# Hybrid recurrent decoder step: pairwise products alternate between two heads, two last stores on another queue, stage order changed

## The chip, the cores and the metric

One core of one Trainium2 chip runs the whole program. The metric is device microseconds of one execution. The kernel before was timed three times: 1033.18, 1036.73 and 1042.99 us, median 1036.73 us.

## The reference

One layer over a prompt of 1024 tokens and 8 single-token samples, all in float32. Each branch below has 4 heads of 64 channels, and is a causal recurrence.

```python
h = rms_norm(x, norm_g)
proj = jnp.matmul(h, w_in)            # split into the columns of four branches
o_gla  = gla_mix(q, k, v, log_a, s0)  # gated linear attention
y_s5   = s5_mix(u, ...)               # diagonal complex state space
o_gdn  = gdn_mix(q, k, v, g, beta, s0)        # gated delta net, triangular solve per 64 tokens
o_rwkv = rwkv7_mix(r, log_w, k, v, kk, a, s0) # RWKV-7
mixed = jnp.concatenate([o_gla, o_s5, o_gdn, o_rwkv]) * silu(gates)
out = rms_norm(x + mixed @ w_out, final_g)    # and the new states of every branch
```

## The kernel before, in words

The prompt is worked in two halves of 512 tokens; the second half (marked `'` in the order string) also carries the 8 sample tokens. A branch's four heads are two pairs; a pair is a *unit*, written as a generator with stages: `R` (RWKV, `rwkv_unit`), `D` (delta net, `gdn_unit`), `L` (GLA, `gla_unit`), `g` (gates), `S` (S5), `W` (weights of S5). Two heads of a pair lie on partitions 0 to 63 and 64 to 127 (`HS[0]`, `HS[1]`).

**Projections.** `stream` (L278 to L287) multiplies a 128-column weight tile with the normed tokens. Values are split in a high and a low part, so each weight block costs three matmuls of L286: `hi*hi`, `hi*lo`, `lo*hi`. In the first half a projection called before `rwkv_lora` has run is cut into two pieces of 256 columns (`X["pieces"]`, set at L129 and cleared at L418); later ones have one piece of 512. In the second half the pieces are 260 columns.

**Pairwise products.** Each of the three matrix branches builds token-by-token products per head, from 64 partitions of that head:
- RWKV, L472: for each of four blocks `b`, a PSUM tile from the pool `psb` (two tiles, tag "b"), four matmuls of one head, then a mask multiply on VectorE (L473).
- Delta net, L684: for each head a tile, eight matmuls, then a VectorE multiply (L685).
- GLA, L785 to L802: on each of six levels, for each head a tile, matmuls (L791 for the levels of 64 and 32, L794 for 16, 8, 4, 2), then ScalarE copies (L798) or VectorE predicated copies (L802).
In float32 a matmul of these is recorded as two instructions, so four matmuls of the text are x8 in the profile.

**Recurrences.** After the products a unit inverts triangular blocks (`inverse`, L296: VectorE steps L319 and L321, small DMAs, products L338, L342, L351, L356), and then steps through its chunks one after another with a 128x128 state: L515 for RWKV (eight matmuls of the program for a chunk, the state update is L531), L721 for the delta net, L851 for GLA.

**What sets the order.** `ORDER` (L33) lists stages; the loop at L1411 issues them, each under a priority offset from `PRI` (L32, by unit letter and stage number: `R1` is stage 1 of an RWKV unit, which holds L472). Within that, the tile framework orders each engine's instructions itself, by priorities and a model of when operands and buffers come free. So a few characters of the string move instructions on all engines. An engine then runs its list strictly in that order. The second half's tokens are loaded and normed by token `x'`: its transposes (L256) write into the buffers that hold the first half's tokens, so they follow the last L286 of the first half.

**The end.** `tail` (L1351) scales four row blocks of 128 tokens and one of 8, alternately on ScalarE and VectorE, and stores each (L1393) on the queue of SyncE.

Of the kernel before, what the change touches and what calls it, by code (L numbers as in the profile page):

```python
# [12 lines left out]
ALU = mybir.AluOpType  # L13
# [17 lines left out]
           rU="V", dU="V", fg="V", la="V", tlo="V", cv0="V")  # L31
PRI = {"R2": 1875, "D2": 1000, "R3": 4000, "D3": 2000, "L1": 1600, "R1": 600, "L0": 100, "L2": 600, "D0": 150, "D1": 1250}  # L32
ORDER = ("x W W t R0 m D0 W W g6 R0 W W W M D0 D1 R1 R0 R1 L0 R1 R0 L0 R1 D1 L0 g0 S g0 L1 D0 D0 g4 g6 D1 g3 g7 g2 L1 L1 D1 x' "  # L33
         "g7 g1 g5 g4 S t' R1' R1' g2 R1' m' R0' g3 M' R1' g1' g7' R0' D0' R0' D0' L1' D1' g1 g5 R0' D0' D1' g4' g6' D0' L0' L1' "
         "g2' L1' D1' g7' g0' D1' L0' g6' S' g4' L0' g5' g3' S' g5' g3' g0' g1' g2' T y T'")
GORD = ((RWKV, 0), (RWKV, 1), (GDN, 0), (GDN, 1), (GLA, 0), (GLA, 1), (S5, 0), (S5, 1))
# [27 lines left out]
def trunk(ctx: ExitStack, tc: tile.TileContext, I, O):  # L64
# [35 lines left out]
    def psb(*shape):  # L100
        return ps_b.tile(list(shape) or [128, 512], F32, tag="b", name="psb")
# [10 lines left out]
    def act(out, in_, func, scale=1.0, bias=0.0, **kw):  # L112
        A.activation(out, in_, func, bias=bias, scale=scale, **kw)  # L113
# [293 lines left out]
    def rwkv_unit(h, pair, th):  # L407
# [59 lines left out]
        Gt = [big(128, 8, 128, name="Gt") for _ in range(2)]  # L467
        for b in range(4):
            e, c0 = b % 2, 4 * (b // 2)
            pg = psb(128, 4, 128)  # L470
            for j in range(4):
                PE.matmul(pg[:, j, :], BK[HS[e], c0 + j, :], AR[HS[e], c0 + j, :], start=True, stop=True)  # L472
            gt = V.tensor_tensor(Gt[b // 2].rearrange("p (c e f) t -> p e c (f t)", f=2, e=2)[:, e], pg.rearrange("p (c f) t -> p c (f t)", f=2),  # L473
                                 maskG.rearrange("p (o t) -> p o t", o=1).to_broadcast([128, 2, 256]), ALU.mult)
        yield
# [170 lines left out]
    def gdn_unit(h, pair):  # L646
# [32 lines left out]
        act(Gt, Gt, AF.Exp)  # L679
        act(kdn, kdn, AF.Exp)  # L680
        for e in range(2):
            pg = psb(128, 4, 128)
            for c in range(8):
                PE.matmul(pg[HS[c % 2], c // 2, :], kx[HS[e], 64 * c:64 * c + 64], SK[HS[e], c, :], start=True, stop=True)  # L684
            gt = V.tensor_tensor(G4[:, e], pg, G4[:, e], ALU.mult)  # L685
        yield
# [60 lines left out]
    def gla_unit(h, pair, sm):  # L747
# [26 lines left out]
        for lv, s in enumerate((64, 32) + LEVELS[:-1]):  # L774
# [9 lines left out]
            tt("lw1", wv[:, :, 1, :], v4(qx)[:, :, 1, :], dv[:, :, 1, :])  # L784
            for e in range(2):  # L785
                pg = psb(128, 4, 64)
                for c in range(4):
                    if s >= 32:
                        for b in range(64 // s):
                            o = 128 * c + 2 * s * b  # L790
                            PE.matmul(pg[2 * s * b:2 * s * b + s, c, 0:s], W[HS[e], o:o + s], W[HS[e], o + s:o + 2 * s], start=True, stop=True)  # L791
                    else:
                        t = slice(128 * c, 128 * c + 128)
                        PE.matmul(pg[:, c, :], W[HS[e], t], W[HS[e], t].rearrange("p (b f s) -> p f b s", f=2, s=s)[:, 1], start=True, stop=True)  # L794
                if s >= 32:
# [555 lines left out]
    def tail(fgb):  # L1351
# [36 lines left out]
        for x, j, k in rows:  # L1388
            if j % 2 or j == 4:
                V.tensor_scalar(x, x, y[:k, j:j + 1], None, ALU.mult)  # L1390
            else:
                act(x, x, AF.Copy, scale=y[:k, j:j + 1])
            SP.dma_start(out=O["y"][HALF + 128 * j:HALF + 128 * j + k, :], in_=x)  # L1393

# [192 lines left out]
```

## Time and profile before

| | |
|---|---|
| median of three runs | 1036.73 us |
| profiled execution | 1045.8 us |
| its span | 1043.7 us |
| PE matmul busy | 931.7 us, 89% of the span |
| VectorE busy | 604.4 us, 58% |
| ScalarE busy | 474.7 us, 45% |
| GpSimd busy | 290.2 us, 28% |
| mean granted TensorE clock | 0.873 of 2.4 GHz |

PE is the engine that is busy nearly all the time. Its matmuls are pipelined, so its busy time counts a stretch as busy in which matmuls follow each other, whatever their rate. The profiled execution is 0.9% longer than the median, and ahead of all three timed runs.

### The profile page before, as it was taken

The numbers are of one execution on the slowest core, as the hardware profiler recorded it, in microseconds if no ns is written. First come the engines' busy times: TensorE is split into PE (matmuls) and PEld (weight loads), VectorE is DVE, ScalarE is ACT, GpSimd is POOL, SyncE is SP. The second block draws the span as 40 slices with busy tenths as digits, with TensorE's granted clock in tenths as the row PEclk, the third lists the DMA queues.
The fourth block names the chain that finished last, engine by engine and source line by source line (L and its number), as shares of the span: only waits on it lengthen the run. The fifth ranks groups of instructions, "written<-read, shape, count | busy, mean of one in ns | idle before, by whom it ended". The sixth has DMA issues, their size and how long they took to land.

```text
span 1043.7 us, 19159 instructions
## 1 busy us (share of the span) xinstructions
PE 931.7 (89%) x7018; PEld 759.9 (73%) x7018; DVE 604.4 (58%) x1619; ACT 474.7 (45%) x1128; POOL 290.2 (28%) x355
## 2 busy tenths in 40 slices
PE   3899869989999899798999899999999989897795
PEld 3577646768767687588778778878878968785694
DVE  8512987465646655844375768856664564726523
ACT  4335455333374443532572655636244254267233
POOL 2696853442121360021010201013304302430000
PEclk9899977976998885599998999969898879799698
DMA  8356434331222342135344424523232256547643
GB/s 257 97 204 189 132 102 117 96 92 44 81 75 92 109 140 81 49 115 182 92 143 114 133 84 103 175 43 107 54 114 89 84 162 189 173 151 246 229 155 111
DMA packets 107774, 130.66 MB, mean 125 GB/s; under 512 B 44841, under 2 KB 56241, under 8 KB 107681
## 3 DMA queue, kind: packets, MB, share of 16 engines
q1 hardware_dynamic: 107680, 129.44, 40.5%
q8 instruction: 55, 0.90, 0.4%
q14 instruction: 39, 0.31, 0.1%
HBM read 91.68 MB, written 35.60 MB: 122 GB/s over the span
## 4 chain that ended last, share of the span: by engine, by line
PE 64%; DVE 16%; DMA 7%; ACT 6%; issue 3%; POOL 3%; SPq 2%; ACTq 0%; DVEq 0%; POOLq 0%
PE psp L286 35%; PE psc L515 5%; PE psc L721 3%; PE psb L794 3%; DMA wl<-wk 2%; PE psb L815 1%; PE psc L851 1%; POOL wl L273 1%; DVE DT L321 1%; PE psb L472 1%; PE psb L227 1%; DVE DP L319 1%; DMA constB<-in_constB 1%; PE psb L1180 1%; PE psb L1181 1%
## 5 line engine op out<-in xcount | busy, mean ns | idle before, releaser
L286 PE MATMUL psp<-xhi,wl 128*128 128x260 f32 (+2 forms) x728 | 251.7, 349 | 8.6 <-POOL wl L273 5.7
L286 PE MATMUL psp<-xhi,wh 128*128 128x260 f32 (+2 forms) x728 | 255.4, 351 | 4.0 <-DVE gp L1250 1.9
L286 PE MATMUL psp<-xlo,wh 128*128 128x260 f32 (+2 forms) x728 | 247.4, 340 | 0.9 <-DVE xlo L258 0.9
L286 PEld LDWEIGHTS psp<-xhi,wl 128*128 128x128 f32 x728 | 146.4, 202 | 29.7 <-POOL wl L273 8.5
L286 PEld LDWEIGHTS psp<-xhi,wh 128*128 128x128 f32 x728 | 147.8, 203 | 26.3 <-issue 6.5
L269 ACT CAST wh<-wr 128x512 fp32r<-128x512 f32 x152 | 93.6, 617 | 145.9 <-PE psp L286 101.4
L286 PEld LDWEIGHTS psp<-xlo,wh 128*128 128x128 f32 x728 | 147.8, 203 | 15.0 <-issue 2.7
L273 POOL TENSOR_TENSOR wl<-wr,wh 128x512 fp32r<-128x512 f32 x76 | 101.2, 1333 | 186.1 <-ACT wh L269 153.5
L286 PE MATMUL psp<-olo,wh 128*128 128x260 f32 (+1 forms) x192 | 65.2, 340 | 6.5 <-DVE olo L117 6.1
L286 PE MATMUL psp<-ohi,wh 128*128 128x260 f32 (+1 forms) x192 | 65.7, 346 | 4.8 <-ACT ohi L1299 4.7
L286 PE MATMUL psp<-ohi,wl 128*128 128x260 f32 (+1 forms) x192 | 64.3, 341 | 1.8 <-DMA wl<-wk 1.8
L286 PEld LDWEIGHTS psp<-olo,wh 128*128 128x128 f32 x192 | 38.6, 201 | 10.7 <-DVE olo L117 7.5
L286 PEld LDWEIGHTS psp<-ohi,wh 128*128 128x128 f32 x192 | 37.9, 199 | 8.2 <-ACT ohi L1299 5.5
L286 PEld LDWEIGHTS psp<-ohi,wl 128*128 128x128 f32 x192 | 38.1, 201 | 4.8 <-DMA wl<-wk 2.2
L515 PE MATMUL psc<-UV,Gt 64*64 64x64 f32 (+1 forms) x256 | 38.8, 282 | 2.7 <-ACT UV L508 1.4
L113 ACT ACTIVATE eg<-eg 128x260 f32<-128x260 f32 (+1 forms) x72 | 33.3, 484 | 16.2 <-DVE eg L200 15.5
L515 PEld LDWEIGHTS psc<-UV,Gt 64*64 64x64 f32 (+1 forms) x256 | 29.6, 182 | 11.4 <-issue 4.8
L117 POOL TENSOR_TENSOR df<-cum 128x256 f32<-128x256 f32 x48 | 30.5, 655 | 20.4 <-DVE DT L321 9.3
L319 DVE TENSOR_TENSOR DP<-DT,LT 128x30 f32<-128x30 f32 (+10 forms) x120 | 31.6, 263 | 7.9 <-DMA LT<-d 4.9
L794 PE MATMUL psb<-W 64*128 64x64 f32 x256 | 35.6, 321 | 0.0
L794 PEld LDWEIGHTS psb<-W 64*128 64x128 f32 x256 | 31.7, 226 | 3.1 <-issue 0.9
L256 PE MATMUL psb<-constA,xn 128*128 128x128 f32 (+1 forms) x72 | 16.6, 387 | 19.3 <-DVE xlo L258 9.8
(441 smaller groups left out, 1890.3 us busy)
## 6 DMA issues: line engine op xcount, KB each, us to landing
wr<-in_wct SPq DMA_DIRECT2D x120, 256.0 KB
wk<-wl SPq DMA_DIRECT2D x76, 256.0 KB
wl<-wk SPq DMA_DIRECT2D x76, 256.0 KB
wr<-in_wo SPq DMA_DIRECT2D x32, 256.0 KB
xn<-in_x SPq DMA_DIRECT2D x8, 512.0 KB
dgp<-gp SPq DMA_DIRECT2D x8, 256.0 KB
Gml<-dG SPq DMA_DIRECT2D x4, 512.0 KB
csT<-dph SPq DMA_DIRECT2D x4, 512.0 KB
```

The source lines that it names most:

```text
L113: A.activation(out, in_, func, bias=bias, scale=scale, **kw)
L117: return (G if ENG[name] == "G" else V).tensor_tensor(out, a, b, op)
L227: PE.matmul(p, bones, t, start=True, stop=True)
L256: PE.transpose(pt[:, k, :n], xn[:n, (4 * b + k) * 128:(4 * b + k + 1) * 128], ident[:n, :n])
L269: A.copy(hi, raw)
L273: G.tensor_tensor(lo, raw, hi, ALU.subtract)
L286: X["mm"] = PE.matmul(p[:, :m], w[:, k % 4, :], x[:, k, c0:c0 + m], start=(i == 0 and s == 0), stop=(i == 7 and s == 2))
L319: V.tensor_tensor(tp[:, :m, :w], DT[:, :m, j:j + 1].to_broadcast([128, m, w]), LT[:, j:j + 1, j + 1:16].to_broadcast([128, m, w]), ALU.mult)
L321: V.tensor_tensor(DT[:, :m, j + 1:16], DT[:, :m, j + 1:16], tp[:, :m, :w], ALU.add)
L515: PE.matmul(o, l, r, start=start, stop=True, skip_group_check=True)
L721: PE.matmul(o, l, r, start=start, stop=True, skip_group_check=True)
L794: PE.matmul(pg[:, c, :], W[HS[e], t], W[HS[e], t].rearrange("p (b f s) -> p f b s", f=2, s=s)[:, 1], start=True, stop=True)
```

## The change

The three products are rewritten. Both heads' PSUM tiles are taken first (`pgs`, two tiles, which is the whole pool `psb`), and the matmuls then go head 0, head 1, head 0, head 1; the evacuations of both tiles follow. The number and the shapes of matmuls stay. In `tail` the stores of row blocks 0 and 2 are issued by ScalarE, which has scaled them; the other three stay on SyncE. `PRI["R1"]` goes from 600 to 1200, and `ORDER` is changed at some twelve places: the small projection `m` moves ahead of `t` (so it now runs as two pieces of 256 columns, 48 matmuls in place of 24), `M` and the first `R1` move ahead of the last `W W`, `g6`, `L1` and `D1` change places in the first half, `R1'` runs four times in a row, and `L1'` moves up.

```diff
-PRI = {"R2": 1875, ..., "R1": 600, "L0": 100, "L2": 600, "D0": 150, "D1": 1250}
-ORDER = ("x W W t R0 m D0 W W g6 R0 W W W M D0 D1 R1 R0 R1 L0 R1 R0 L0 R1 D1 L0 g0 S g0 L1 D0 D0 g4 g6 D1 ...
+PRI = {"R2": 1875, ..., "R1": 1200, "L0": 100, "L2": 600, "D0": 150, "D1": 1250}
+ORDER = ("x m W W t R0 D0 W W g6 R0 W M D0 R1 W W R0 R1 L0 R1 R0 L0 R1 D1 L0 D1 g0 S g0 D0 D0 g4 D1 ...
@@ rwkv_unit
-        for b in range(4):
-            e, c0 = b % 2, 4 * (b // 2)
-            pg = psb(128, 4, 128)
+        for b in range(2):
+            pgs = [psb(128, 4, 128) for _ in range(2)]
             for j in range(4):
-                PE.matmul(pg[:, j, :], BK[HS[e], c0 + j, :], AR[HS[e], c0 + j, :], start=True, stop=True)
-            gt = V.tensor_tensor(Gt[b // 2]...[:, e], pg..., maskG..., ALU.mult)
+                for e in range(2):
+                    PE.matmul(pgs[e][:, j, :], BK[HS[e], 4 * b + j, :], AR[HS[e], 4 * b + j, :], start=True, stop=True)
+            for e in range(2):
+                gt = V.tensor_tensor(Gt[b]...[:, e], pgs[e]..., maskG..., ALU.mult)
@@ gdn_unit
+        pgs = [psb(128, 4, 128) for _ in range(2)]
+        for c in range(8):
+            for e in range(2):
+                PE.matmul(pgs[e][HS[c % 2], c // 2, :], kx[HS[e], 64 * c:64 * c + 64], SK[HS[e], c, :], start=True, stop=True)
         for e in range(2):
-            pg = psb(128, 4, 128)
-            for c in range(8):
-                PE.matmul(pg[HS[c % 2], c // 2, :], kx[HS[e], 64 * c:64 * c + 64], SK[HS[e], c, :], start=True, stop=True)
-            gt = V.tensor_tensor(G4[:, e], pg, G4[:, e], ALU.mult)
+            gt = V.tensor_tensor(G4[:, e], pgs[e], G4[:, e], ALU.mult)
@@ gla_unit
-            for e in range(2):
-                pg = psb(128, 4, 64)
-                for c in range(4):
-                    ...
+            pgs = [psb(128, 4, 64) for _ in range(2)]
+            for c in range(4):
+                for b in range(64 // s if s >= 32 else 1):
+                    for e in range(2):
+                        pg = pgs[e]
+                        ...
+            for e, pg in enumerate(pgs):
+                ...
@@ tail
-            SP.dma_start(out=O["y"][HALF + 128 * j:HALF + 128 * j + k, :], in_=x)
+            (SP if j % 2 or j == 4 else A).dma_start(out=O["y"][HALF + 128 * j:HALF + 128 * j + k, :], in_=x)
```

The lines after the first edit are shifted by up to four: L515, L721 and L794 of before are L516, L723 and L797 of the changed kernel.

The first place is PE's list at the first GLA unit of the first half, on the level of 16. The number behind `psb` is the PSUM tile: one for each head. Before:

```order
L794 MATMUL psb_2368<-W_2361 128x64 x4
L351 MATMUL psi_2018<-Dn_2088,Gt_1777 32x32 x7
L351 MATMUL psi_2018<-Dn_2088,Gt_1778 32x32 x8
L794 MATMUL psb_2374<-W_2361 128x64
L515 MATMUL psc_2265<-state30_119,AR_977 128x128
L794 MATMUL psb_2374<-W_2361 128x64 x2
```

And now:

```order
L797 MATMUL psb_2262<-W_2255 128x64
L797 MATMUL psb_2263<-W_2255 128x64
L797 MATMUL psb_2262<-W_2255 128x64
L797 MATMUL psb_2263<-W_2255 128x64
L797 MATMUL psb_2262<-W_2255 128x64
L797 MATMUL psb_2263<-W_2255 128x64
```

The two heads' matmuls, which stood apart, now take turns. On PE's whole list this is so for 12 of the 16 groups of L794 (three GLA units of four), for 4 of the 8 groups of L472 (one of the four mostly), and, nearly throughout, for the 4 groups of L684.

The second place is the second GLA unit of the first half, whose last levels stand between the last projections of the first half and the transposes of `x'`. Before:

```order
L794 MATMUL psb_3887<-W_3880 128x64 x4
L794 MATMUL psb_3893<-W_3880 128x64 x4
L721 MATMUL psc_3365<-state20_115,KQ_1217 128x128
L710 MATMUL psc_3380<-constA_82,raw1_706 128x128
L711 MATMUL psc_3380<-constA_82,raw2_750 128x128
L794 MATMUL psb_3906<-W_3899 128x64 x4
L794 MATMUL psb_3912<-W_3899 128x64 x4
```

And now:

```order
L797 MATMUL psb_3913<-W_3906 128x64 x4
L797 MATMUL psb_3914<-W_3906 128x64 x4
L286 MATMUL psp_4427<-xhi_140,wl_4422 128x512
L286 MATMUL psp_4427<-xhi_140,wh_4421 128x512
L286 MATMUL psp_4427<-xlo_141,wh_4421 128x512
...
L797 MATMUL psb_3932<-W_3925 128x64 x4
L797 MATMUL psb_3933<-W_3925 128x64 x4
```

Here the framework has put four of one head ahead of four of the other, as before; but ten projections (L286) now stand between the first two levels, where before none was left. Between the last L286 of the first half and the first transpose of `x'` there were 114 matmuls, and there are 64.

The third place is the first RWKV unit's recurrence, where PE's list had projections between the chunks. Before:

```order
L515 MATMUL psc<-UV,Bn 128x128
L515 MATMUL psc<-UV,Gt 64x64 x2
L286 MATMUL psp<-xhi,wh 128x512
L286 MATMUL psp<-xlo,wh 128x512
L286 MATMUL psp<-xhi,wl 128x512
```

And now:

```order
L516 MATMUL psc<-UV,Bn 128x128
L516 MATMUL psc<-UV,Gt 64x64 x2
L516 MATMUL psc<-state_119,AR 128x128
L503 MATMUL psc<-constA,BK 128x128 x2
L505 MATMUL psc<-constA,rx_641 64x128
L506 MATMUL psc<-constA,rx_641 64x128
L794 MATMUL psb<-W 64x64 x8
L516 MATMUL psc<-r,XT 64x64 x2
```

Chunk follows chunk with little else between. Between the 16th and the 64th L515 there were 55 projections and there are 25. In return more projections stand ahead of the recurrence: the last product of the first inverse (L356) has 444 L286 ahead of it before, and 483 of the same work now (507, less the 24 that the cut of `m` adds); in the second half the second inverse of an RWKV unit has 1600 and 1704.

## Rows read from the trace of the kernel before

**Rows 1.** Stretches: length, busy us (count) of PE, PEld, DVE, ACT, POOL; clock, DMA.
```profile
234.00:286.00 52.00, 52.00 (x487) 41.52 (x486) 32.10 (x83) 17.58 (x47) 10.43 (x10) 0.81 0.21 58
728.00:754.00 26.00, 26.00 (x247) 22.86 (x246) 15.51 (x39) 7.56 (x19) 10.29 (x15) 0.90 0.25 66
806.00:832.00 26.00, 26.00 (x198) 24.02 (x198) 12.99 (x33) 7.33 (x19) 11.90 (x15) 0.91 0.35 105
...
379.00:441.00 62.00, 53.32 (x328) 44.78 (x323) 43.06 (x119) 27.41 (x71) 10.81 (x16) 0.56 0.17 55
```
**Rows 2.** Chain of waits, share by line, in 240:275, 728:750 and 806:828.
```profile
by line: PE psp L286 26.7%; PE psb L794 26.3%; PE psc L515 24.9%; PE psb L815 5.6%; PE psi L356 3.9%; PE psc L504 2.5%; PE psc L502 2.4%; PE psi L351 2.3%; PE psi L342 2.0%; PE psb L791 1.5%; PE psb L833 1.4%; PE psc L505 1.0%; PE psi L338 
by line: PE psp L286 37.0%; PE psb L794 32.4%; PE psc L515 8.8%; PE psc L721 8.4%; PE psb L815 7.6%; PE psi L338 4.0%; PE psb L791 2.4%; PE psc L711 0.5%; PE psc L710 0.5%
by line: PE psp L286 36.0%; PE psb L794 32.2%; PE psc L851 19.2%; PE psc L721 11.5%; PE psc L710 1.2%; PE psc L711 0.5%
```
**Rows 3.** Timeline of PE and of its weight loads: start us, us, what.
```profile
156.22 1.22 PE L419 MATMUL psb<-rx,constB 64*128 64x512 f32 x1 [0.79 <-DVE Gg L685]
156.23 1.11 PE L515 MATMUL psc<-UV,Gt 64*128 64x64 f32 x4
...
156.22 0.28 PEld L419 LDWEIGHTS psb<-rx,constB 64*128 64x128 f32 x1 [1.19 <-DVE Gg L685]
156.22 0.28 PEld L515 LDWEIGHTS psc<-UV,Gt 64*128 64x128 f32 x1
```
**Rows 4.** Timeline of PE: groups of the products.
```profile
268.63 1.10 PE L794 MATMUL psb<-W 64*128 64x64 f32 x8
...
745.64 1.61 PE L794 MATMUL psb<-W 64*128 64x64 f32 x16
...
129.18 1.16 PE L472 MATMUL psb<-AR,BK 64*128 64x128 f32 x8
...
386.15 2.88 PE L794 MATMUL psb<-W 64*128 64x64 f32 x16
```
**Rows 5.** L472 alone in two stretches (PE, PEld, clock, DMA); L684 by line.
```profile
183.00:194.00 11.00, 3.42 (x32) 3.04 (x32) 1.00 0.34 101
538.00:552.00 14.00, 5.86 (x32) 5.08 (x32) 0.71 0.28 76
...
L684 PE MATMUL psb<-SK,raw 64*64 64x128 f32 x128 | 10.3, 350 | 4.8 <-ACT SK L662 4.8
```
**Rows 6.** Groups by line on VectorE: evacuations (busy us, mean ns | idle before).
```profile
L802 DVE COPY_PREDICATED At<-lmask,psb 128x256 f32<-128x256 uint8 x32 | 15.9, 509 | 14.5 <-PE psb L794 10.8 <-ACT UV L508 2.4 <-ACT on L735 0.9
L473 DVE TENSOR_TENSOR Gt<-psb,constB 128x512 f32<-128x512 f32 x16 | 10.8, 684 | 14.3 <-PE psb L472 14.2
```
**Rows 7.** Timeline of PE around `x'`; waits of SyncE's queue.
```profile
378.14 0.40 PE L286 MATMUL psp<-xhi,wl 128*128 128x512 f32 x1
...
407.73 1.91 PE L256 MATMUL psb<-constA,xn 128*128 128x128 f32 x8
...
441.23 0.58 PE L286 MATMUL psp<-xhi,wh 128*128 128x260 f32 x1
...
SPq L138 <- PE psc L721: 23.6, 2, 22.7
```
**Rows 8.** Timeline of PE in the front: a wait for a weight tile.
```profile
42.99 0.80 PE L286 MATMUL psp<-xhi,wl 128*128 128x512 f32 x1 [3.30 <-POOL wl L273]
```
**Rows 9.** L286 alone by stretch: 512 columns, then 260 (PE, clock, DMA).
```profile
78.00:104.00 26.00, 23.68 (x101) 1.00 0.60 187
...
988.00:1014.00 26.00, 24.46 (x189) 1.00 0.50 162
```
**Rows 10.** Timeline of VectorE: the first RWKV unit's first state update.
```profile
200.85 0.58 DVE L531 SCALAR_TENSOR_TENSOR state<-psc,fx,state 64x64 f32<-64x64 f32 x2
```
**Rows 11.** Engines in the last stretch; timeline of the last stores' issues.
```profile
1036.50:1042.00 5.50, 0.00 (x0) 0.00 (x0) 0.58 (x1) 0.69 (x1) 0.00 (x0) 0.50 0.99 387
...
1035.80 2.87 SPq L1393 DMA_DIRECT2D out_y<-xf  x4
```

More of the change, by code (lines that the diff above doesn't have):

```diff
@@ L31 @@
            rU="V", dU="V", fg="V", la="V", tlo="V", cv0="V")
[L32 to L35, printed above, removed]
+PRI = {"R2": 1875, "D2": 1000, "R3": 4000, "D3": 2000, "L1": 1600, "R1": 1200, "L0": 100, "L2": 600, "D0": 150, "D1": 1250}
+ORDER = ("x m W W t R0 D0 W W g6 R0 W M D0 R1 W W R0 R1 L0 R1 R0 L0 R1 D1 L0 D1 g0 S g0 D0 D0 g4 D1 g3 g7 g2 L1 g6 L1 L1 D1 x' "
+         "g7 g1 g5 g4 S t' R1' R1' R1' R1' g2 m' R0' g1' g7' L1' R0' g3 M' D0' R0' D0' D1' g1 g5 R0' D0' D1' g4' g6' D0' L0' L1' "
+         "g2' L1' D1' g7' g0' D1' L0' g6' S' g4' L0' g5' g3' S' g0' g1' g5' g3' g2' T y T'")
 GORD = ((RWKV, 0), (RWKV, 1), (GDN, 0), (GDN, 1), (GLA, 0), (GLA, 1), (S5, 0), (S5, 1))
@@ L467, in rwkv_unit @@
         Gt = [big(128, 8, 128, name="Gt") for _ in range(2)]
-        for b in range(4):
-            e, c0 = b % 2, 4 * (b // 2)
-            pg = psb(128, 4, 128)
+        for b in range(2):
+            pgs = [psb(128, 4, 128) for _ in range(2)]
             for j in range(4):
-                PE.matmul(pg[:, j, :], BK[HS[e], c0 + j, :], AR[HS[e], c0 + j, :], start=True, stop=True)
-            gt = V.tensor_tensor(Gt[b // 2].rearrange("p (c e f) t -> p e c (f t)", f=2, e=2)[:, e], pg.rearrange("p (c f) t -> p c (f t)", f=2),
-                                 maskG.rearrange("p (o t) -> p o t", o=1).to_broadcast([128, 2, 256]), ALU.mult)
+                for e in range(2):
+                    PE.matmul(pgs[e][:, j, :], BK[HS[e], 4 * b + j, :], AR[HS[e], 4 * b + j, :], start=True, stop=True)
+            for e in range(2):
+                gt = V.tensor_tensor(Gt[b].rearrange("p (c e f) t -> p e c (f t)", f=2, e=2)[:, e], pgs[e].rearrange("p (c f) t -> p c (f t)", f=2),
+                                     maskG.rearrange("p (o t) -> p o t", o=1).to_broadcast([128, 2, 256]), ALU.mult)
         yield
@@ L784, in gla_unit @@
             tt("lw1", wv[:, :, 1, :], v4(qx)[:, :, 1, :], dv[:, :, 1, :])
-            for e in range(2):
-                pg = psb(128, 4, 64)
-                for c in range(4):
-                    if s >= 32:
-                        for b in range(64 // s):
+            pgs = [psb(128, 4, 64) for _ in range(2)]
[3 more added lines that the diff above has]
+                        pg = pgs[e]
+                        if s >= 32:
                             o = 128 * c + 2 * s * b
                             PE.matmul(pg[2 * s * b:2 * s * b + s, c, 0:s], W[HS[e], o:o + s], W[HS[e], o + s:o + 2 * s], start=True, stop=True)
-                    else:
-                        t = slice(128 * c, 128 * c + 128)
-                        PE.matmul(pg[:, c, :], W[HS[e], t], W[HS[e], t].rearrange("p (b f s) -> p f b s", f=2, s=s)[:, 1], start=True, stop=True)
+                        else:
+                            t = slice(128 * c, 128 * c + 128)
+                            PE.matmul(pg[:, c, :], W[HS[e], t], W[HS[e], t].rearrange("p (b f s) -> p f b s", f=2, s=s)[:, 1], start=True, stop=True)
+            for e, pg in enumerate(pgs):
                 if s >= 32:
```

## The prediction

> **What bounds the kernel now.** I read the page's busy shares first, then busy time and the chain of waits by stretch, since an average of 89% for PE says nothing of where a product counts. In the three stretches that hold GLA products after which this change reaches, PE is busy for all of the 52, 26 and 26 us, while no other engine passes 62% of a stretch [rows 1]. The chain inside them has only PE lines: L794 is 26.3% of 35 us, 32.4% of 22 us and 32.2% of 22 us, that is 9.2, 7.1 and 7.1 us, together 23.4 us [rows 2]. So in those places a shorter product is a shorter kernel, until another engine's step becomes the slower one.
>
> **Products that take turns.** The trace of before has one place where matmuls of the two partition halves meet: a matmul of L419 and four of L515. Both weight loads begin at 156.22, and the four instructions of L515 run from 156.23 while the first of L419 takes until 157.44; they do not queue behind it [rows 3]. So halves run side by side, each at its own pace. One head's eight instructions of L794 take 1.10 us; both heads, one after the other, 1.61 us at the full clock, and 2.88 us [rows 4] in the stretch 379:441, whose mean granted share is 0.56 [rows 1]. The 1.61 is less than twice 1.10 because the second head starts while the first one's last instructions are still queued. A group that takes turns should cost one head's time, 1.10 us.
>
> - L794: twelve of sixteen groups take turns in PE's list, all in the three stretches above. 12 times 1.10 is 13.2 us in place of 23.4: 10.2 us off the chain. The bounds are nothing (the halves don't overlap in this shape) and twice that, if groups now scattered between other matmuls also save the pieces of idle around them.
> - The other four groups, 380 to 393 us, where a group costs 2.88 us, stay one head after the other (the second place shown in the change). I count nothing for them.
> - L472: four of eight groups, in the stretches with 3.42 and 5.86 us of it [rows 5]. At 1.16 us for one head [rows 4] they cost 4.6 us, 4.6 less. L684: all four groups, 10.3 us [rows 5]; by halves 5.1 less. L791 I leave at nothing. These 9.7 us lie mostly beside a VectorE chain or a wait, so I take about a third: 3 us; bounds 0 and 9.7.
>
> Sum of the products: 13 us (0 to 23).
>
> What follows each group is its evacuation: two copies of 0.51 us for L794, two mask multiplies of 0.68 us for L472 [rows 6]. Both tiles of the pool are now held until then; the next user of a `psb` tile waits for the first copy. Before, at the groups that ran as x16, both tiles were held as well, so I count nothing for it.
>
> The Trainium skill (TensorEngine Tiling, section Performance Considerations, PSUM Bottleneck) says that such packing speeds up TensorE and leaves the evacuation as it was, so that the copy may become the limit. By that rule a group of L472 would cost two multiplies, 1.37 us in place of 1.16, and the products would give 12 to 13 us instead of 13; for L794, 1.02 us of copies stay just under 1.10. No run here shows it yet; its stronger form is the first rival.
>
> **The stretch before the second half's tokens.** The last L286 of the first half is at 378.14 us, the first transpose of `x'` at 407.73, the next L286 at 441.23 [rows 7]. In these 63 us PE runs small matmuls, mostly at the lower of the clock's two levels, 1.2 GHz: the mean granted share is 0.56 [rows 1]. The changed order leaves 64 matmuls where 114 stood ahead of the transposes, and moves the other 50 among projections. By share of 29.6 us that is 13 us of PE time, which costs about half at the full clock (1.61 against 2.88 for the same group [rows 4]): 6 us. But the loads of `x'` wait 22.7 us on the delta net's chain (L721) for their buffers [rows 7], so not all of it can pass. I take 4 us; bounds 0 and 10.
>
> **The front.** PE waits 3.30 us for a weight tile of GpSimd [rows 8]. `m` ahead of `t` puts some 6 us of projections before that point (24 matmuls of 512 columns at 23.68/101 or 0.234 us are 5.6 us; the 48 of 256 columns that they become, at 24.46/189 or 0.13 us of 260 columns, 6.2 [rows 9]). They can cover the wait, or can delay `t` and the first RWKV unit behind it. I take 2 us of gain; bounds 3.3 gained and 6.2 lost.
>
> **The recurrences.** They run one after another, and the first state update is at 200.85 us [rows 10]. In the changed list 39 more projections stand ahead of the first inverse's last product, at most 39 times 0.234 us [rows 9] or 9.1 us, and fewer stand inside the recurrence. Where PE was idle or waiting before the inverse they cost nothing, and the PE work left behind them shrinks by as much. I take 0; bounds 10 gained and what the last rival costs lost.
>
> **The last stores.** SyncE issues four stores in 2.87 us; two now go out from ScalarE, which saves some 1.4 us of issue (half of 2.87). But from 1036.5 to 1042 the stores move 387 GB/s with the DMA engines 99% busy [rows 11]: 2 MB take 5.4 us at that rate, and start no earlier. ScalarE also issues behind both of its scalings. I take 0; bounds 0 and 1.4 gained.
>
> **Sum.** 13 + 4 + 2 + 0 + 0 is 19 us. Against the profiled execution of 1045.8 us that is 1026.8. That execution is 9 us above the median of the three runs, 1036.7, and the terms are differences, so against the median I forecast 1018 us.
>
> **Rivals.**
> 1. *The freed PE time goes idle.* A GLA level needs exponents on ScalarE, four products on GpSimd and VectorE, the matmuls, and copies. If that sequence or its copies set the pace, the 13 us vanish and 6 us of order remain: 1031 us. For it: L802 waited for L794 10.8 us in all [rows 6], so copies follow products closely. Against it: in these stretches the chain has only PE lines [rows 2], and VectorE is at 60 of 104 us [rows 1]. The rule of the Trainium skill cited above (PSUM Bottleneck) would end this way in its stronger form; the trace of before doesn't bear it out there, since PE is busy for the whole of those stretches.
> 2. *Turns don't overlap on the chip in these shapes*: again 1031 us. Against it stand [rows 3]; what speaks for it is that there the two streams were of different lines and widths, and no row shows equal ones in turns.
> 3. *The RWKV recurrence comes late and bare: slower.* The place is the inverse ahead of it. First half: 9.1 us later, and 30 fewer projections (55 to 25) inside the recurrence, 7.0 us of cover that is lost where a chunk's ScalarE and VectorE steps set the pace. Second half: the second inverse has 104 more projections of 260 columns ahead of it, at 0.13 us [rows 9] 13.5 us. Against a gain of 19 that is 29.6 us lost; and if the later recurrences then run bare too, so that PE waits in the GLA stretches as well, the products' 13 us don't count either: 1036.7 - 6 + 29.6, or 1060 at the worst, 1047 with the products. I put it at 1050. It decides from the point where the first state update (L531) is more than 19 us later than 200.85. Against it: PE idles or waits before the inverse, so the projections moved there fill holes.
>
> **How the numbers follow.** The forecast's chance is 0.62, with its own range of 1006 to 1030 (the products from 5 to 23 us, the order from 2 to 8). Rival 1 has 0.19, rival 2 has 0.06, rival 3 has 0.13. A measurement of this kernel can tell about 1% from no change, so faster means below 1026, slower above 1047. About an eighth of the forecast's cases lies above 1026, and a quarter of those of rival 1 below: faster 0.59, the same 0.29, slower 0.12. The range of 8 in 10 is 1002 to 1038: it takes in rivals 1 and 2 with their spread and leaves out rival 3 and the best cases, where the stretch before `x'` and the recurrences give all of their bounds.
>
> **What would show it.** Right: groups of L794 as x16 in about 1.1 us at the full clock, with starts of both heads' instructions in turns; fewer than 25 us of L794 on PE in all; a stretch without L286 before `x'` under 58 us; the first state update near 200 us; the last stores ending as before after their first issue. Wrong: a group in turns that still takes 1.6 us (rival 2); PE's busy share in the three GLA stretches clearly under 100% with VectorE or GpSimd as releasers (rival 1); the first state update beyond 219 us, or L515 with idle time on VectorE and ScalarE in the recurrence (rival 3).

## The result and the profile after

The changed kernel takes 1025.59 us (median of four runs, 1023.61 to 1031.28), the kernel before 1039.86 over its four runs. The ratio is 0.9864, with a 95% interval of 0.9822 to 0.9906: 1.4% or 14.3 us faster. Ratios and means here and below take in only runs within about 1.5% of the fastest of the same kernel, the medians given in us all of them. The forecast was 1018 us in a range of 1002 to 1038; it named a gain of 18.7 us.

The page of the changed kernel, busy time by engine (share of the span, instructions):

```profile
span 1025.4 us, 19223 instructions
PE 913.5 (89%) x7042; PEld 743.1 (72%) x7042; DVE 602.3 (59%) x1619; ACT 474.5 (46%) x1129; POOL 290.9 (28%) x355
```

The share of PE is still 89%; the profiled span is 18.3 us shorter, and PE is 18.2 us less busy (931.7 to 913.5). Where? The first question is answered by stretches cut at the first projection of the second half (L286 with 260 columns), which is at 441.23 us before [rows 7] and here:

```profile
440.59 0.58 PE L286 MATMUL psp<-xhi,wh 128*128 128x260 f32 x1
```

So of the gain of this execution 0.6 us has come by then, and the rest comes behind it. Six of the kernels tried below have the changed kernel's list on PE up to that point; they get there between 438.4 and 446.0 us, so the 0.6 can't be told from nothing. The stretches up to there, and from there to the last matmul (length, busy us and count of PE, PEld, DVE, ACT, POOL, clock, DMA); first before:

```profile
0.00:441.20 441.20, 383.77 (x2644) 290.81 (x2644) 268.87 (x725) 196.09 (x429) 186.95 (x222) 0.84 0.38 114
441.20:1031.20 590.00, 547.96 (x4375) 469.04 (x4374) 331.24 (x882) 274.40 (x685) 101.14 (x128) 0.90 0.43 133
```

and after:

```profile
0.00:440.60 440.60, 386.40 (x2669) 294.50 (x2669) 266.38 (x725) 197.13 (x430) 184.87 (x222) 0.82 0.38 114
440.60:1012.20 571.60, 527.10 (x4375) 448.62 (x4374) 331.69 (x882) 273.17 (x685) 103.89 (x128) 0.92 0.45 137
```

In the second half PE does the same 4375 matmuls, is idle for 44.5 us in place of 42.0, and is busy for 20.9 us less; its clock is higher. The product groups themselves did what was forecast. PE's rows by line, before:

```profile
L794 PE MATMUL psb<-W 64*128 64x64 f32 x256 | 35.6, 321 | 0.0
L472 PE MATMUL psb<-AR,BK 64*128 64x128 f32 x128 | 18.0, 309 | 1.4 <-DVE Gt L473 1.4
```

(L684 is in [rows 5], 10.3 us), and after (L685 is L684 of before):

```profile
L797 PE MATMUL psb<-W 64*128 64x64 f32 x256 | 25.2, 315 | 0.0
L472 PE MATMUL psb<-AR,BK 64*128 64x128 f32 x128 | 13.5, 292 | 1.2 <-DVE bv L456 1.2
L685 PE MATMUL psb<-SK,raw 64*64 64x128 f32 x128 | 7.7, 307 | 1.9 <-ACT SK L663 1.9
```

That is 10.4, 4.5 and 2.6 us less. Four groups on the timeline of PE, which answer to [rows 4]: one in turns at 2.4 GHz, one in turns at 1.2 GHz, and one of the unit where the framework left four of a head ahead of four of the other, at 2.4 GHz and at 1.2:

```profile
718.50 1.11 PE L797 MATMUL psb<-W 64*128 64x64 f32 x16
...
239.80 1.97 PE L797 MATMUL psb<-W 64*128 64x64 f32 x16
...
381.01 1.60 PE L797 MATMUL psb<-W 64*128 64x64 f32 x16
...
389.77 3.37 PE L797 MATMUL psb<-W 64*128 64x64 f32 x16
```

Both heads in turns take 1.11 us, what one head took alone (1.10). The halves do run side by side.

**A way to add up the second half.** For each kernel the trace gives PE's idle time from the first projection of the second half to the last matmul, and the part of its busy time that lies at the lower clock level, 1.2 GHz (summed over the records of the clock). A busy microsecond at 1.2 GHz counted as half one at 2.4 gives a rest, the work at full clock. For before: 590.0 - 42.0 idle - 106.1/2 = 494.9. For after: 571.6 - 44.5 - 73.5/2 = 490.4. So of the 18.4 us that the second half became shorter, 16.3 are time at the low clock, 4.5 are work, and 2.5 more were idle. The experiments all go into this table:

| kernel | second half starts | length | idle | busy at 1.2 GHz | rest |
|---|---|---|---|---|---|
| before | 441.2 | 590.0 | 42.0 | 106.1 | 494.9 |
| after | 440.6 | 571.6 | 44.5 | 73.5 | 490.4 |
| e1, products alone | 440.1 | 590.9 | 42.8 | 119.6 | 488.3 |
| e2, order and stores alone | 438.3 | 593.3 | 50.2 | 103.1 | 491.5 |
| e3, first half's order as before | 438.7 | 571.7 | 41.5 | 74.4 | 493.0 |
| e4, second half's order as before | 438.4 | 606.8 | 45.3 | 138.3 | 492.3 |
| e5, priority 600 | 442.6 | 571.3 | 45.4 | 70.7 | 490.5 |
| e6, all stores on SyncE | 446.0 | 568.2 | 45.8 | 63.9 | 490.4 |
| e7, GLA products as before | 454.0 | 613.4 | 55.8 | 134.5 | 490.3 |
| f7, e7 with 24 matmuls added | 454.0 | 589.2 | 50.5 | 91.1 | 493.1 |
| e8, RWKV and delta net products as before | 443.5 | 602.5 | 43.9 | 127.7 | 494.8 |
| e10, one GLA stage back | 441.5 | 581.6 | 43.2 | 97.7 | 489.6 |
| e12, RWKV stages back | 444.6 | 599.6 | 49.6 | 121.6 | 489.2 |
| fa, after with 24 matmuls added | 438.5 | 578.9 | 42.5 | 84.8 | 494.0 |

The rest keeps within 7 us, while the lengths lie 45 us apart, and follow the time at 1.2 GHz. It is one execution each, and the counting by half is rough. How rough shows in after, e5 and e6, which have the same list on PE: 73.5, 70.7 and 63.9 us at 1.2 GHz. But runs of one and the same kernel say the same: over 20 runs of before, whose instructions are the same each time, the span goes from 1029.7 us at a mean clock of 0.889 to 1044.9 us at 0.871, with a correlation of -0.97.

The table leaves out the first half, and that changes the picture. Up to the first projection of the second half the work at full clock is 7.4 us less after the change (321.6 to 314.2), but 20.1 us more are busy at 1.2 GHz (124.4 to 144.5), which takes 10.0 of it back. Over the whole kernel the work is 11.9 us less (816.5 to 804.6), and the time at 1.2 GHz 12.6 us less (230.5 to 217.9), worth 6.3. The means over runs say so without any cut: span times mean clock, a rough measure of the time at full clock, is 910 us for before (43 runs) and 901 for the changed kernel (10 runs, with those of e5, which is the same program), the mean clock 0.875 and 0.879. So most of the gain is saved work, done at about the clock of before.

### The profile page after: what moved, and what is told of

Its sections match the earlier page's. It is cut to its first block, busy times and chain, and to the rows that moved or that the text cites. A ratio compares the mean times of both kernels' runs of the same rounds, so it can differ in the third digit from the quotient of the medians.

```text
span 1025.4 us, 19223 instructions
## 1 busy us (share of the span) xinstructions
PE 913.5 (89%) x7042; PEld 743.1 (72%) x7042; DVE 602.3 (59%) x1619; ACT 474.5 (46%) x1129; POOL 290.9 (28%) x355
## 4 chain that ended last, share of the span: by engine, by line
PE 67%; DVE 17%; DMA 6%; ACT 4%; issue 3%; POOL 2%; SPq 1%; DVEq 0%; ACTq 0%; POOLq 0%
PE psp L286 37%; PE psc L516 6%; PE psc L723 4%; DMA wl<-wk 2%; PE psb L797 2%; DVE DP L319 2%; PE psc L855 2%; DVE DT L321 1%; PE psb L819 1%; PE psb L472 1%; PE psi L338 1%; DMA constB<-in_constB 1%; PE psb L227 1%; DMA rot<-sX 1%; DVE acc L619 1%
## 5 line engine op out<-in xcount | busy, mean ns | idle before, releaser
L286 PE MATMUL psp<-xhi,wh 128*128 128x260 f32 (+2 forms) x736 | 254.1, 346 | 9.5 <-DVE rx L387 5.9
L286 PE MATMUL psp<-xhi,wl 128*128 128x260 f32 (+2 forms) x736 | 251.3, 345 | 7.7 <-DMA wl<-wk 5.2
L286 PE MATMUL psp<-xlo,wh 128*128 128x260 f32 (+2 forms) x736 | 247.8, 338 | 0.9 <-DVE xlo L258 0.9
L286 PEld LDWEIGHTS psp<-xhi,wh 128*128 128x128 f32 x736 | 148.0, 201 | 29.7 <-DVE rx L387 5.0
L286 PEld LDWEIGHTS psp<-xhi,wl 128*128 128x128 f32 x736 | 147.1, 201 | 28.4 <-DMA wl<-wk 6.4
L286 PEld LDWEIGHTS psp<-xlo,wh 128*128 128x128 f32 x736 | 148.0, 201 | 13.7 <-issue 1.4
L286 PE MATMUL psp<-olo,wh 128*128 128x260 f32 (+1 forms) x192 | 64.9, 338 | 5.7 <-DVE olo L117 4.7
L286 PE MATMUL psp<-ohi,wh 128*128 128x260 f32 (+1 forms) x192 | 65.8, 345 | 1.0 <-ACT ohi L1303 1.0
L286 PE MATMUL psp<-ohi,wl 128*128 128x260 f32 (+1 forms) x192 | 64.8, 343 | 1.7 <-DMA wl<-wk 1.7
L286 PEld LDWEIGHTS psp<-olo,wh 128*128 128x128 f32 x192 | 38.7, 202 | 9.2 <-DVE olo L117 5.5
L286 PEld LDWEIGHTS psp<-ohi,wl 128*128 128x128 f32 x192 | 38.4, 202 | 4.9 <-DMA wl<-wk 2.1
L286 PEld LDWEIGHTS psp<-ohi,wh 128*128 128x128 f32 x192 | 38.2, 200 | 4.1 <-ACT ohi L1303 1.3
L516 PE MATMUL psc<-UV,Gt 64*128 64x64 f32 (+1 forms) x256 | 40.0, 293 | 0.0
L516 PEld LDWEIGHTS psc<-UV,Gt 64*128 64x128 f32 (+1 forms) x256 | 30.7, 191 | 8.4 <-issue 2.5
L256 PE MATMUL psb<-constA,xn 128*128 128x128 f32 (+1 forms) x72 | 16.4, 384 | 21.5 <-DVE xn L252 10.8
L736 DVE SCALAR_TENSOR_TENSOR state<-state,egb,psc 64x64 f32<-64x64 f32 x64 | 17.9, 279 | 26.3 <-PE psc L723 25.3
L532 DVE SCALAR_TENSOR_TENSOR state<-psc,fx,state 64x64 f32<-64x64 f32 x64 | 18.1, 282 | 22.3 <-PE psc L516 21.3
```

What stands on the lines that cost most here:

```text
L286: X["mm"] = PE.matmul(p[:, :m], w[:, k % 4, :], x[:, k, c0:c0 + m], start=(i == 0 and s == 0), stop=(i == 7 and s == 2))
L516: PE.matmul(o, l, r, start=start, stop=True, skip_group_check=True)
L532: V.scalar_tensor_tensor(Sbd[hp, hp], pc[hp, 256 + 64 * e:320 + 64 * e], fx[hp, 1, c:c + 1], Sbd[hp, hp], ALU.mult, ALU.add)
L736: V.scalar_tensor_tensor(Sbd[hp, hp], Sbd[hp, hp], egb[hp, 64 * c + 63:64 * c + 64], pc[hp, 256 + 64 * e:320 + 64 * e], ALU.mult, ALU.add)
```

## The experiments

Each was timed beside the kernel before on its own chip: e1 to e4, e7, e8, e10 and e12 on one, e5, e6, f7 and fa on another. Across the two, compare the ratios to before and not the microseconds.

**First question: is it the products or the order?**

e1 is the kernel before with the three new product loops only; e2 the changed kernel with the old loops.

> The kernel before with the three product loops rewritten and nothing else (order, priorities and stores as before). Theory A (the products carry most of the gain, as the prediction's sum has it, 13 of 19 us): 1023 to 1030 us. Theory B (the freed TensorE time goes idle and the order carries the gain): 1034 to 1040 us. In its list 7 of the 16 groups of the four small levels take turns wholly or nearly, and every group of the delta net; the second half's groups mostly in parts (AAABBBAB), so by the trace of after, where a group in turns takes 1.1 us and one of four and four about 1.6, A itself gives no more than 8 us.

Measured: 1043.40 us against 1043.28, ratio 1.0004 (0.9965 to 1.0043).

> The changed kernel with the old product loops (order, priorities and stores as changed). Theory A: it loses what the products give, 1031 to 1037 us. Theory B: it keeps the gain, 1022 to 1029 us.

Measured: 1050.86 us, ratio 1.0106 (1.0053 to 1.0159).

Neither theory holds. The products alone give nothing, the order alone loses 1.1%, and both together gain 1.4%. In e1 the rows of the products are shorter by 4.9 us (L797), 0.1 (L472) and 2.3 (L685):

```profile
L797 PE MATMUL psb<-W 64*128 64x64 f32 x256 | 30.7, 317 | 1.8 <-DVE At L806 1.3 <-POOL W L117 0.5
L472 PE MATMUL psb<-AR,BK 64*128 64x128 f32 x128 | 17.9, 324 | 0.2 <-DVE bv L456 0.2
L685 PE MATMUL psb<-SK,raw 64*64 64x128 f32 x128 | 8.0, 352 | 1.1 <-ACT SK L663 1.1
```

In the table its rest is 6.6 us under that of before, as these 7.3 us would have it, and its busy time at 1.2 GHz is 13.5 us longer, which costs 6.8. The gain did not go idle; it went into the clock. One execution would not show this, since 13.5 us is little more than the same list varies by, but the runs do: over 12 each, the mean clock is 0.868 in e1 and 0.877 in before, and span times clock 903 and 911 us. One place shows how it looks: 741 to 761 us, where the end of a GLA unit (the last group of L797, then L819 and L837, the next steps of the unit) meets the small 32x32 products of a delta net inverse (L338). The stretch in before, and in e1:

```profile
741.00:761.00 20.00, 20.00 (x178) 16.82 (x178) 10.94 (x24) 5.63 (x13) 2.88 (x3) 0.74 0.17 46
```

```profile
741.00:761.00 20.00, 20.00 (x145) 17.31 (x145) 8.02 (x18) 5.01 (x12) 2.86 (x3) 0.50 0.10 28
```

PE is busy for the whole of both, at 0.74 in before and at 0.50, the lower level throughout, in e1; and there 145 matmuls pass in place of 178, with 21 projections among them in place of 31.

**Second question: which half's order?**

e3 puts the part of `ORDER` up to `x'` back as it was, e4 the part behind it:

```diff
 e3: -x m W W t R0 D0 W W g6 R0 W M D0 R1 W W ... L1 g6 L1 L1 D1 x'
     +x W W t R0 m D0 W W g6 R0 W W W M D0 D1 ... g3 g7 g2 L1 L1 D1 x'
 e4: -... t' R1' R1' R1' R1' g2 m' R0' g1' g7' L1' R0' g3 M' D0' R0' D0' D1' ...
     +... t' R1' R1' g2 R1' m' R0' g3 M' R1' g1' g7' R0' D0' R0' D0' L1' D1' ...
```

> The changed kernel with the first half's order (up to the second half's tokens) as before, the second half's as changed. In the traces both kernels are at the same point at 441 us (first projection of the second half at 441.23 and 440.59 us), with all of the gain after that. Theory: the first half's order gives nothing, 1022 to 1029 us, and the first projection of the second half stays within 2 us of 441. Rival (the products' gain in the first half shows once the bare recurrence is gone): that projection comes by 436 us or earlier, and the time is 1015 to 1021 us. Second rival (the first half's order sets up the second): 1032 to 1038 us.

Measured: 1027.16 us, ratio 0.9851 (0.9794 to 0.9907). The theory's time holds: the first half's order (the early `m`, `R1` ahead of `W W`, the moved gates) gives nothing that can be told. Its mark was just missed: the first projection of the second half is at 438.7 us, 2.3 from 441 where within 2 was asked.

> The changed kernel with the second half's order as before. In its list the second half's eight groups of the small levels stand four and four again. Theory (all of the gain lies in the second half and comes with its order, which also lets the groups take turns): 1033 to 1040 us. Rival (the products as rewritten give it whatever the order): 1023 to 1029 us.

Measured: 1061.47 us, ratio 1.0206 (1.0163 to 1.0249). That is slower than both ranges. Without the second half's order the whole gain is gone, and the kernel is 2% slower than before. By the table that is again the clock: 138.3 us at 1.2 GHz, while the rest is 492.3. With the order went the turns, though: in e4's list all eight groups of the small levels in the second half stand four and four.

**Third question: which products, in the new order?**

e7 has the GLA products as before, e8 the other two.

> The changed kernel with the GLA products alone as before (RWKV and delta net in turns, order as changed). In the runs so far a kernel's span times its granted clock hardly moves from run to run (910 us for before, 903 with the three products alone, 907 with the order alone), and the span follows the clock. Theory (the GLA groups are the larger part of the products' 7 us at full clock): the product of span and clock rises by 3 to 6 us against the changed kernel's 899, and the time by more if the clock falls too: 1030 to 1042 us. Rival (RWKV and delta net carry it): 1023 to 1029 us.

Measured: 1081.30 us, ratio 1.0363 (1.0318 to 1.0408), outside the range of both theories. In the profiled executions 13.4 us of the loss have come by the first projection of the second half (454.0 after 440.6).

> The changed kernel with the RWKV and delta net products as before and the GLA products in turns. Theory: 1 to 3 us more at full clock, 1025 to 1031 us. Rival (these carry the part that the order alone lost): 1035 to 1045 us.

Measured: 1053.24 us, ratio 1.0107 (1.0060 to 1.0154), above the rival's range too, which ended at 1045.

These can't be added: e2, with all three undone, is faster than e7 with one undone. A change of the program can also make the framework order the lists of all engines anew. But e7 has a place that tells more than its time. In the changed kernel the first GLA unit of the second half runs its four small levels between 718 and 734 us, mostly in turns and at 2.4 GHz. In e7, one head after the other, the same levels (L796 there) take from 748 to 779 us:

```profile
748.00:792.00 44.00, 44.00 (x188) 38.22 (x188) 17.02 (x45) 8.32 (x19) 9.17 (x12) 0.50 0.12 29
```

The clock fell to 1.2 GHz at 747.8 us, after PE had run the 32x32 products of L356 and three projections, and had waited 1.77 us for a state update on VectorE (L532). It rose again at 792. In these 44 us PE was busy throughout, with products of one head, the 16 of L817, a few chunks, and 57 projections spread among them.

**Fourth question: is the low clock a cost, or only the mark of a place where PE waits anyway?**

f7 is e7 with 24 matmuls that nobody needs, in the row ahead of those levels; fa is the changed kernel with the same. In these two kernels the added line is L788 and L787. They write a PSUM tile that the products then overwrite:

```diff
-                pg = psb(128, 4, 64)
+                pg = psb(128, 4, 64); [PE.matmul(pg.rearrange("p c t -> p (c t)"), X["hi"][:, r % 8, 0:128], X["hi"][:, r % 8, 0:256],
+                    start=True, stop=True) for r in range(24 if h == 1 and pair == 1 and s == 16 and e == 0 else 0)]
```

> The changed kernel with the GLA products as before, and 24 matmuls of 256 columns added that nobody reads (their PSUM tile is overwritten by the products), ahead of the first level-16 group of the second half's first GLA unit. Up to that place TensorE's list is the same as without them. Without them the clock fell to 1.2 GHz at 747.8 us, and stayed there until 792 us through products of one head, a few projections and chunks. Theory (the low clock is itself a cost, and a dense block of work brings it back): the stretch at 1.2 GHz from there is under 15 us in place of 44, and the time falls by 8 us or more, 1081 to 1073 or less, although work was added. Rival (the low clock only marks a place where TensorE waits anyway): the stretch stays at 30 us or more, or the time is the same or up to 6 us longer.

Measured: 1058.21 us, ratio to before 1.0127 (1.0091 to 1.0163), where e7 has 1.0363 (1.0318 to 1.0408): over 2% less time, though work was added. The timeline of PE at the block:

```profile
741.59 0.80 PE L516 MATMUL psc<-state,AR 128*128 128x128 f32 x2 [1.78 <-DVE state L532]
742.04 3.33 PE L788 MATMUL psb<-xhi 128*128 128x256 f32 x14
...
745.45 1.84 PE L788 MATMUL psb<-xhi 128*128 128x256 f32 x7
747.22 0.69 PE L516 MATMUL psc<-r,XT 64*64 64x64 f32 x4
747.84 0.62 PE L788 MATMUL psb<-xhi 128*128 128x256 f32 x3
748.39 1.16 PE L796 MATMUL psb<-W 64*128 64x64 f32 x12
```

The same wait stands ahead of it (1.78 us), and the clock falls there as in e7, at 741.0. At 747.8, near the block's end, it is back, and the stretch of the GLA levels behind it reads

```profile
748.00:765.00 17.00, 17.00 (x134) 14.70 (x134) 9.64 (x25) 5.05 (x11) 5.22 (x8) 1.00 0.13 36
```

134 matmuls in 17 us at 1.00, against 188 in 44 us at 0.50; each stretch holds all 64 instructions of L796. The stretch at 1.2 GHz is 6.8 us long, where the theory asked for under 15. In the table f7 has 43.4 us less at 1.2 GHz than e7, which counts for 21.7 us, and is idle for 5.3 less; the rest is 2.8 us larger, the price of the 24 matmuls. That makes the 24.2 us by which its second half is shorter. Not all of it is due to the block: with the same list up to there, f7's execution came to the wait 6.0 us earlier (741.59 against 747.61). Behind the block 18.2 us are left, and there the two lists differ, so the stretch at the block is the cleaner evidence, and the whole time the weaker.

> The changed kernel with the same 24 added matmuls at the same place, where it already runs at 2.4 GHz. Theory: there is no low stretch to win back, so it costs the 24 matmuls (at 0.11 us, 2.7 us) or more if the list behind them falls out of its order: 1027 to 1045 us. Rival (added matmuls help wherever they stand): 1020 us or less.

Measured: 1029.40 us, ratio 0.9843 (0.9799 to 0.9888), in the theory's range: where no low stretch is to be won back, the block gains nothing. In its trace the 24 matmuls take 3.12 us, 0.13 us each. Its time can't be told from that of the changed kernel (ratios 0.9843 and 0.9864).

**Fifth question: which tokens of the second half?**

e10 puts one GLA stage back behind the delta net's, e12 the RWKV stages of the second pair back among the gates:

```diff
 e10: -R0' g1' g7' L1' R0' g3 M' D0' R0' D0' D1' g1 g5
      +R0' g1' g7' R0' g3 M' D0' R0' D0' L1' D1' g1 g5
 e12: -R1' R1' R1' R1' g2 m' R0' g1' g7' L1' R0' g3 M' D0'
      +R1' R1' g2 R1' m' R0' g3 M' R1' g1' g7' L1' R0' D0'
```

> The changed kernel with one token back in its old place in the second half: the first GLA product stage behind the delta net's stages. In its list the first GLA unit's four groups of the small levels then stand four and four, those of the second unit still take turns. Theory (the order works by putting the groups in turns): about 2 us at full clock lost, 1027 to 1034 us. Rival (the order works by where projections lie, which this token hardly moves): within 3 us of the changed kernel. Second rival (this move is the larger part of the second half's order): 1038 us or more.

Measured: 1039.77 us, ratio 0.9988 (0.9952 to 1.0024): the whole gain is gone, with one token; the second rival.

> The changed kernel with the second half's RWKV stages and gates interleaved as before (the GLA stage kept early). Theory: the second inverse then has the cover of before, and TensorE's clock falls as there in the stretch of the delta net's products and inverse (683 to 704 us in before, 3.4 us in after): 1030 to 1040 us at a mean clock of 0.87. Rival (the place of the RWKV stages costs nothing, as the prediction's third rival feared a loss from it): 1020 to 1028 us.

Measured: 1053.28 us, ratio 1.0075 (1.0028 to 1.0123), slower than the theory's range. Its trace is of a long execution (1058.9 us), so the sizes in it are upper ones.

Both lose by the same mark: over their runs span times clock is 900 us in e10 and in e12, where the changed kernel has 901, while the mean clock is 0.867 and 0.860 in place of 0.879. The stretches of the GLA unit's end, in e10 and in e12:

```profile
725.00:749.00 24.00, 24.00 (x104) 20.70 (x105) 8.51 (x20) 5.81 (x13) 2.72 (x3) 0.51 0.14 44
```

```profile
749.00:783.00 34.00, 34.00 (x148) 28.98 (x148) 14.77 (x34) 5.93 (x14) 3.85 (x5) 0.50 0.15 42
```

24 and 34 us at the low level, PE busy throughout, with 26 and 49 projections among L797, L819, L837 and chunks. In the changed kernel the stretch of the same unit reads

```profile
710.00:735.00 25.00, 25.00 (x233) 22.59 (x234) 15.36 (x44) 10.38 (x25) 11.38 (x15) 0.86 0.27 83
```

233 matmuls in 25 us, 84 of them projections. The moved tokens put projections among the unit's products, and among the delta net's products and inverse ahead of them, 677 to 704 us in before (29 projections) and 676 to 704 in after (89). First before, then after:

```profile
677.00:704.00 27.00, 25.08 (x191) 20.06 (x190) 14.04 (x34) 11.31 (x30) 2.89 (x2) 0.63 0.25 51
```

```profile
676.00:704.00 28.00, 26.63 (x334) 22.04 (x334) 19.19 (x48) 16.80 (x45) 6.85 (x7) 0.94 0.35 87
```

One thing is not separated. In PE's lists the groups of the small levels of that same unit, the first GLA unit of the second half, are in turns, wholly or for the most part, in after, e5, e6 and fa, and but for one group in e3, all at ratios of 0.983 to 0.986. They stand four and four, or nearly, in every kernel that gains nothing or loses: e1, e2, e4, e7, e8, e10, e12 and f7; e2, e7 and e8 among them have the whole new order. So the tokens may work through the turns, through the projections among the products, or through both. That turns are not needed for the clock there is shown by f7, whose unit runs at 1.00 with its groups four and four.

**The small parts.**

> The changed kernel with the priority offset of the RWKV product stage as before, 600 in place of 1200. The first half's list is the same; in the second half the RWKV products and what stands around them move. Theory (the time of this kernel hangs on how its list falls, and any other list loses clock): 1032 to 1045 us at a mean clock of 0.87 or less, with the product of span and clock still near 900. Rival (the offset is of no account, as the prediction left it at nothing): 1022 to 1029 us.

Measured: 1027.20 us, ratio 0.9826 (0.9796 to 0.9856), in the rival's range. But nothing moved, against what the text above expects: e5 has the same lists as the changed kernel on every engine, and its trace has the same 7042 matmuls in the same order. So the priority is of no account here, and the theory that any other list loses clock was not tested by it. What e5 gives is a second set of runs of the changed kernel.

> The changed kernel with all five last stores on SyncE again. From the last matmul to the end of the span, before took 12.5 us and the runs with ScalarE's stores 12.9 to 13.3. Theory: those stores give nothing, and all on SyncE the end is 0.3 to 0.7 us shorter: 1023 to 1028 us, the same within what can be told. Rival (the prediction's bound of 1.4 us gained): the stretch behind the last matmul is 14 us or more, and the time 1026 to 1030 us.

Measured: 1029.95 us, ratio 0.9863 (0.9829 to 0.9897): the time is 2 us above the theory's range, but the ratio is that of the changed kernel, 0.9864. From the last matmul to the end it is 12.9 us, 0.3 less than after, as the theory had it. The stores on ScalarE give nothing that can be told.

## Why the prediction was right, and where it was not

The time lay in the range, and the direction and the size of the gain were right. The sum behind it was right only in part: its largest term came, but under a condition that the prediction did not name, and its other 6 us did not come. That the total still ended 4.4 us from the forecast of the gain is in part luck.

**Products at PE: right in the main.** 10.2 + 4.6 + 5.1, 19.9 us, were worked out for PE itself; 10.4 + 4.5 + 2.6, 17.5, came, the delta net's part at half its size. A group in turns takes 1.11 us, as forecast, and L797 takes 25.2 us in all, where under 25 was the mark. The prediction's bounds for the products, 0 to 23, are not those of its terms, which add up to 30.1 (20.4 and 9.7). Rival 2 fell. The evacuations stayed as they were: L806 14.9 us (15.9 for L802 in [rows 6]), L474 10.6 (10.8). To this extent the trace agrees with the rule cited from the Trainium skill (TensorEngine Tiling, Performance Considerations, PSUM Bottleneck); its stronger form didn't come, since in the second half's product stretches the chain of waits still has only PE lines, which answers to [rows 2] (share by line in 711:735 and 786:806):

```profile
by line: PE psp L286 56.4%; PE psb L797 20.1%; PE psc L516 15.5%; PE psc L723 4.5%; PE psb L794 4.2%; PE psc L712 0.5%; PE psc L713 0.5%
by line: PE psp L286 45.4%; PE psb L797 21.5%; PE psc L855 19.5%; PE psc L723 12.9%; PE psc L712 0.6%; PE psc L713 0.6%
```

**Products at the end: the step that failed.** "So in those places a shorter product is a shorter kernel, until another engine's step becomes the slower one." e1 refutes it as it stands: its products are 7.3 us shorter on PE, and its time is the same. The prediction looked for the loss in another engine's pace (rival 1, 1031 us); PE's own clock took it, 0.868 over the runs in place of 0.877. In the changed kernel the saved work (901 us of span times clock in place of 910) does reach the end, at a clock of 0.879; e2, with the order alone, has 907 us at 0.864. That PE is busy for 100% of a stretch does not say how much it gets done there: 145 matmuls or 178 in the same 20 us.

**The stretch before `x'`: wrong in size, 4 us, 0.6 came, within the spread.** The mark was fulfilled: from the last projection of the first half (385.31 us) to the next one (440.59) it is 55.3 us, where under 58 was asked, after 63.1. But the stretch became shorter at its front, and its end stayed. It hangs on the first half's delta net, which lets the loads of `x'` go (SyncE's longest wait for it is 22.7 us before, 14.5 after); the last update of its first unit:

```profile
411.02 0.57 DVE L734 SCALAR_TENSOR_TENSOR state<-state,egb,psc 64x64 f32<-64x64 f32 x2 [0.88 <-PE psc L721]
```

before, and after:

```profile
410.38 0.57 DVE L736 SCALAR_TENSOR_TENSOR state<-state,egb,psc 64x64 f32<-64x64 f32 x2
```

**The recurrences: 0 was right for the first half's sum, but two effects are in it.** The first state update came at 198.97 us (near 200 as forecast), and the last RWKV update 9.9 us earlier (331.88 to 321.97). The recurrence ran bare, as rival 3 said, and PE's clock fell there, before and after, 200 to 330 us:

```profile
200.00:330.00 130.00, 122.30 (x1048) 94.69 (x1048) 75.56 (x195) 55.70 (x136) 39.87 (x43) 0.86 0.30 87
```

```profile
200.00:330.00 130.00, 117.47 (x967) 90.06 (x967) 81.04 (x242) 55.39 (x135) 30.23 (x34) 0.67 0.19 51
```

81 matmuls fewer pass in that time. 46 of them follow between 330 and 407 us, where PE is now busy for 76.70 of 77 us in place of 71.13, and the delta net's first unit gives back 8.4 of the 9.1 us by which it began earlier. At 0.86 and 0.67 of the clock, 36 and 86 of the 130 us are at 1.2 GHz (2 times 130 times what is missing to 1). The chunks went faster all the same, with fewer projections between them, but the 50 us need not have been free: over the first half 20.1 us more are busy at 1.2 GHz, which counts for 10.0, against 7.4 us of saved work and 3.2 less idle. How much of that is the order's can't be told, since the seven executions with this list have from 123.6 to 144.5 us there. Rival 3's mechanism was there, and its price stayed within that spread.

**The second half's order: the term that was missing.** It was counted within the recurrences at 0. e4, e10 and e12 show that without it the whole gain is gone, through the clock: after has 73.5 us at 1.2 GHz in the second half, these three 97.7 to 138.3. What the order does is to let the saved work count; alone it loses 1.1% (e2). The rows of before showed the means (0.56 in [rows 1], a group at 2.88 us in place of 1.61 in [rows 4]), but the prediction used the clock for one stretch only, and there as a given, not as something that the change would move.

**Front and stores.** The 2 us of the front can't be seen: the wait of 3.30 us for a weight tile is down to 0.61, and one of 4.60 us for `t`'s first values (L387) stands in its place, which answers to [rows 8]:

```profile
33.29 0.39 PE L286 MATMUL psp<-xhi,wl 128*128 128x256 f32 x1 [0.61 <-POOL wl L273]
43.76 0.79 PE L286 MATMUL psp<-xhi,wh 128*128 128x512 f32 x1 [4.60 <-DVE rx L387]
```

e3 shows that undoing it, with the rest of the first half's order, costs nothing. The stores at 0 were right: from the last matmul to the end 13.2 us after, 12.5 before.

**What stays open.** Why a certain list holds the clock and another doesn't is looked at in three places, not derived, and turns and projections were not tried apart; the times of e2, e7 and e8 don't add up, and no part of them is explained but the stretches shown. Whether the two heads need a PSUM bank each wasn't tried.

## What to carry to other kernels

Where an engine is busy for all of a stretch, read its granted clock and the number of instructions that pass, beside its busy share: here the same work took 568 to 613 us with a rest of 488 to 495. A change that shortens small matmuls, or that moves dense ones elsewhere, has to be costed with the clock of the stretch that is left. Dense matmuls among the small products, and behind a wait, are worth a try; f7 is the one run here that tested it by itself. Look at all of the kernel when you add up: a cut at the second half put nearly the whole gain down to the clock, and the whole kernel two thirds of it to saved work. Compare the lists of a variant with its parent's: a priority can move nothing, as in e5. And undo the parts of a tuned change one by one before you believe a sum: here the two parts gave 0 and -1.1% alone, and +1.4% together.

## What was unexpected of the hardware

Useless work made a kernel faster: with 24 matmuls of 256 columns, 3.12 us at full clock in fa, the ratio of e7 to before went from 1.0363 to 1.0127. And a clock that has fallen can stay down as long as only small products and scattered projections run, 44 us in e7, with PE counted as busy for all of it.
